# Batched matrix product on one core: output stores gathered into groups of up to four

## The chip, the cores and the metric

The kernel runs on one core of one Trainium2 chip. The metric is the device time of one launch in microseconds (us), given as the median of several runs. Before the change it is 511.59 us (three runs, 511.37 to 511.65).

The core has five instruction streams: PE (TensorE, matrix products and transposes), DVE (VectorE), ACT (ScalarE), POOL (GpSimd) and SP (SyncE). Transfers between the main memory and the on-chip memory run on 16 DMA engines; POOL and SP put them into queues, and the transfers of one queue are worked through in the order of issue.

## The reference

```python
def setup_inputs():
    batch, m, k, n = 32, 512, 1024, 768
    return {
        "x": np.random.randn(batch, m, k).astype(np.float32),
        "weight": np.random.randn(batch, k, n).astype(np.float32),
    }

def reference(x: np.ndarray, weight: np.ndarray) -> np.ndarray:
    return np.matmul(x, weight).astype(np.float32)
```

There are 32 independent products of 512x1024 by 1024x768. In float32, x is 67.1 MB, weight 100.7 MB and the output 50.3 MB; each byte crosses the memory interface once.

## The kernel before

**Pairs.** The 32 batches are worked in 16 pairs; pair k holds batches 2k and 2k+1. The x of a pair is one transfer of 4.19 MB read (`load_x`, line 111), which POOL issues and which turns float32 into bfloat16 on its way. The weights of a pair are 6.29 MB read, also turned into bfloat16: where `together(b)` holds, one transfer brings both batches (line 98), otherwise there is one transfer for each batch (line 102). The output of a pair is one store of 3.15 MB (`store`, line 119). Store a is the output of pair a.

**Buffers.** There are four slots for weights (two pairs), two for x and four for outputs (`W_SLOTS, X_SLOTS, OUT_SLOTS = 4, 2, 4`). Output slot a % 4 is filled by pair a and is free for pair a + 4 when store a has landed. ACT asks for that (`slot_free`) before the first copy of a pair.

**PE.** For each pair PE transposes the x (`transposes`, line 173, with copies by DVE on lines 219 and 227), then multiplies batch 2k and batch 2k+1 (`multiply`, lines 138 and 165), each in four blocks of 128 rows. A block can only begin when ACT and DVE have emptied the accumulators that it writes (lines 261, 265, 270 and 272). DVE makes its last copy of a pair only behind the transposes of the next pair.

**POOL's order.** POOL's program, `on_pool`, is a plain list. Each step may wait, and everything behind it waits too:

```python
for k in range(PAIRS - 2):
    load_x(k + 2)
    if k % 2 == 0:
        stores(k - 3, k - 1)
    load_w(2 * k + 4)
    load_w(2 * k + 5)
stores(PAIRS - 3 - HELD, PAIRS - 2)
```

`load_x(k + 2)` waits until the first block of pair k is multiplied, since it reuses that pair's x buffer. `stores(first, last)` issues stores first to last-1; each waits for the last copies of its pair. A weight transfer of two batches waits until both batches of pair k are multiplied; one for a single batch waits for one batch. Stores 11, 12 and 13 come at the end of the list. The outputs of the last two pairs are stored by SP: pair 14 in one transfer, batches 30 and 31 in one of half the size each (line 123).

Of the kernel before, what the change touches and what calls it, by code (L numbers as in the profile page):

```python
# [12 lines left out]
def kernel(  # L13
# [7 lines left out]
    B, M, K = x.shape  # L21
# [6 lines left out]
    N2 = 2 * N  # L28
    ROW = MT * N
    PAIRS = B // 2  # L30
    HELD = 2
    GROUPS = 2 * MT
    W_SLOTS, X_SLOTS, OUT_SLOTS = 4, 2, 4

# [53 lines left out]


    def together(b):  # L90
        return W_SLOTS <= b < B - 2

    def load_w(b):
        if together(b):
            if b % 2 == 0:
                pool.wait_ge(s_mm, mm_done(b + 1 - W_SLOTS))
                slots = all_ws[:, b // 2 % 2].rearrange("p r ko n -> p r (ko n)")
                pool.dma_start(out=slots, in_=w_two_view[b // 2]).then_inc(s_w[b % W_SLOTS], 16)  # L98
            return
        if b >= W_SLOTS:  # L100
            pool.wait_ge(s_mm, mm_done(b - W_SLOTS))
        pool.dma_start(out=ws[b % W_SLOTS], in_=w_view[b]).then_inc(s_w[b % W_SLOTS], 16)  # L102

    def loads_of_w(b):

        return sum(not (together(i) and i % 2) for i in range(b % W_SLOTS, b + 1, W_SLOTS))

    def load_x(k):
        if k >= X_SLOTS:
            pool.wait_ge(s_mm, mm_begun(k - X_SLOTS))  # L110
        pool.dma_start(out=xs[k % X_SLOTS], in_=x_view[k]).then_inc(s_x[k % X_SLOTS], 16)  # L111
# [5 lines left out]
    def store(eng, a, sem):  # L117
        copied(eng, 4 * a + 3)
        eng.dma_start(out=two_view[a], in_=outs[a % OUT_SLOTS]).then_inc(sem, 16)  # L119
# [219 lines left out]
    def on_pool():  # L339
        pool.dma_start(out=xs[0][:, MT:], in_=x_view[0, :, MT:]).then_inc(s_rest, 16)  # L340
        load_w(0)
        pool.memset(ident, 0.0).then_inc(s_zero, 1)  # L342
        pool.wait_ge(s_zero, 1)
        pool.affine_select(  # L344
            out=ident,
            in_=ident,
            compare_op=mybir.AluOpType.not_equal,
            fill=1.0,
            base=0,
            pattern=[[-1, P]],  # L350
            channel_multiplier=1,
        ).then_inc(s_ident, 1)
        load_w(1)
        load_x(1)
        load_w(2)
        load_w(3)
        def stores(first, last):
            for a in range(max(first, 0), last):
                store(pool, a, s_st[a % OUT_SLOTS])


        for k in range(PAIRS - 2):
            load_x(k + 2)
            if k % 2 == 0:
                stores(k - 3, k - 1)
            load_w(2 * k + 4)
            load_w(2 * k + 5)
        stores(PAIRS - 3 - HELD, PAIRS - 2)

    def on_sp():  # L370
        for b in range(B):
            if b == 0:
                sp.wait_ge(s_cast, 2).then_inc(s_xr, 1)
            elif b % 2 == 0:
                k = b // 2
                landed(sp, s_x[k % X_SLOTS], (k + 1) // X_SLOTS, s_xr)
            if not (together(b) and b % 2):
                landed(sp, s_w[b % W_SLOTS], loads_of_w(b), s_wr, 1 + together(b))
        store(sp, PAIRS - 2, s_fin)
        store_one(B - 2)  # L380
        store_one(B - 1)
        sp.sem_inc(s_zero, 1)
# [12 lines left out]
    with tc.tile_critical(sync_engine=mybir.EngineType.Activation, no_gpsimd_drain=True):  # L395
        on_pool()
        tc.wait_critical_data_deps()
        on_pe()
        on_dve()
        on_act()  # L400
        on_sp()
        clear_on_pool()
# [30 lines left out]
```

## Time and profile before

| what | value |
|---|---|
| median of the runs | 511.59 us (511.37 to 511.65) |
| span of the profiled execution | 509.6 us, first to last instruction |
| median less that span | 2.0 us, which lie outside the recorded instructions |
| PE, DVE, ACT, POOL busy | 84%, 42%, 22%, 6% of the span |
| transfers issued by POOL | 16 of x, 19 of weights, 14 stores |
| transfers issued by SP | half of the first x, 3 stores |

The profiled execution is given by its span. The profile's busy share of PE is modelled and is not the share of its peak. DMA share is the mean busy share of the 16 DMA engines; since packets overlap a little on an engine, it can read slightly above 1. The view of issues gives, for each transfer, the time from its issue to its landing: a transfer that stands behind others in the queue has their time in it. The moment of landing is the start of the issue in the timeline plus that time.

### The profile page before, as it was taken

To read this page: it belongs to the slowest core of one execution; us is meant where nothing else is said; L and a number is where in the kernel's file an instruction comes from. 1 tells how busy PE (TensorE), PEld (TensorE's weight loads), DVE (VectorE), ACT (ScalarE), POOL (GpSimd) and SP (SyncE) were. 2 spreads that over 40 slices of the span, in tenths; PEclk is the share of its full clock that TensorE was granted. 3 is DMA by queue.
4 is the path that set the end of the run, shared out by engine and by line. 5 is a ranking of instruction groups with operands and counts; after the bars stand their busy time and mean duration, and the time that the engine had idled before them with its cause. 6 is when DMAs were issued, how large, how long until landed. Compare 5 with 4: busy or idle time off the path is not lost. (4 is left out here: it accounts for less than half of the span.)

```text
span 509.6 us, 5832 instructions
## 1 busy us (share of the span) xinstructions
PE 429.4 (84%) x2560; PEld 172.8 (34%) x1536; DVE 211.7 (42%) x330; ACT 114.1 (22%) x195; POOL 29.6 (6%) x55
## 2 busy tenths in 40 slices
PE   0899989999899399993999949999399994999990
PEld 0525342443325034250343513434034341433420
DVE  1436362454635136351373514635146351454631
ACT  1131312223130231302313023230231302223230
POOL 3000000000101001010010100100001000100000
PEclk9999998999999799996999979999699997999996
DMA  8999999999999999999999999999999999999998
GB/s 262 216 211 216 225 207 221 215 305 247 221 212 230 432 234 214 217 237 432 226 215 217 247 433 216 218 217 259 420 217 217 219 267 408 218 215 229 432 430 347
DMA packets 9299, 135.29 MB, mean 266 GB/s; under 512 B 848, under 2 KB 848, under 8 KB 848
## 3 DMA queue, kind: packets, MB, share of 16 engines
q0 software_dynamic: 8720, 126.88, 96.8%
q1 hardware_dynamic: 576, 8.39, 4.0%
q14 instruction: 3, 0.02, 0.0%
HBM read 167.77 MB, written 50.33 MB: 428 GB/s over the span
## 5 line engine op out<-in xcount | busy, mean ns | idle before, releaser
L165 PE MATMUL pm<-w,xT 128*128 x1024 | 346.2, 389 | 42.0 <-DVE outs L270 38.7
L138 PE MATMUL pm<-w,xT 128*128 x1024 | 284.7, 278 | 0.0
L165 PEld LDWEIGHTS pm<-w,xT 128*128 128x128 bf16 x1024 | 102.3, 100 | 282.8 <-issue 241.0
L270 DVE COPY outs<-pm 64x512 f32<-64x512 f32 x128 | 88.2, 689 | 207.7 <-DVEq L268 206.3
L261 ACT COPY outs<-pm 64x512 f32<-64x512 f32 x128 | 74.2, 580 | 272.6 <-PE pm L138 168.4
L173 PE MATMUL pt<-ident,x 128*128 128x128 f32 x512 | 84.5, 307 | 24.8 <-PEq L177 14.5
L219 DVE COPY xT<-pt 128x1024 bf16<-128x1024 bf16 x120 | 77.7, 687 | 63.9 <-PE pt L173 63.6
L173 PEld LDWEIGHTS pt<-ident,x 128*128 128x128 f32 x512 | 71.2, 210 | 40.0 <-DVE xT L219 18.8
L265 ACT COPY outs<-pm 64x512 f32<-64x512 f32 x64 | 37.0, 579 | 99.5 <-PE pm L138 99.3
L272 DVE COPY outs<-pm 64x512 f32<-64x512 f32 x64 | 43.9, 686 | 0.0
L98 POOL DMA_DIRECT2D w<-in_weight_dram x13 | 9.2, 708 | 264.6 <-PE pm L138 264.6
L111 POOL DMA_DIRECT2D x<-in_x_dram x15 | 8.4, 557 | 123.2 <-PE pm L138 92.4
L119 POOL DMA_DIRECT2D out_dram<-outs x14 | 7.5, 539 | 7.1 <-DVE outs L272 7.1
L227 DVE COPY xT<-pt 128x512 bf16<-128x512 bf16 x16 | 5.7, 418 | 4.1 <-PE pt L173 4.1
L280 DVE CAST x<-outs 128x1024 bf16<-128x1024 f32 x2 | 1.3, 692 | 11.0 <-DMA outs<-in_x_dram 11.0
L102 POOL DMA_DIRECT2D w<-in_weight_dram x6 | 3.2, 544 | 26.5 <-PE pm L138 26.3
L280 ACT ACT_TABLE_LOAD x1 | 1.3, 1283 | 10.7 <-DMA outs<-in_x_dram 10.7
L280 ACT CAST x<-outs 128x1024 bf16<-128x1024 f32 x2 | 2.0, 1042 | 0.0
L340 POOL DMA_DIRECT2D x<-in_x_dram x1 | 0.7, 670 | 0.8 <-POOLq L417 0.8
L344 POOL TENSOR_SCALAR_AFFINE_SELECT ident<-ident 128x128 f32<-128x128 f32 x1 | 0.3, 284 | 0.2 <-POOL ident L342 0.2
L342 POOL MEMSET ident<- 128x128 f32 x1 | 0.2, 232 | 0.0
L417 POOL MEMSET const-float32-0.0<- 128x1 f32 x1 | 0.1, 99 | 0.2 <-issue 0.2
(3 smaller groups left out, 0.3 us busy)
## 6 DMA issues: line engine op xcount, KB each, us to landing
out_dram<-outs POOLq DMA_DIRECT2D x14, 3072.0 KB, 40.1
w<-in_weight_dram POOLq DMA_DIRECT2D x13, 3072.0 KB, 32.9
x<-in_x_dram POOLq DMA_DIRECT2D x15, 2048.0 KB, 34.3
w<-in_weight_dram POOLq DMA_DIRECT2D x6, 1536.0 KB, 30.5
out_dram<-outs SPq DMA_DIRECT2D x1, 3072.0 KB, 18.7
out_dram<-outs SPq DMA_DIRECT2D x2, 1536.0 KB, 13.6
outs<-in_x_dram SPq DMA_DIRECT2D x1, 2048.0 KB, 9.7
x<-in_x_dram POOLq DMA_DIRECT2D x1, 1024.0 KB, 11.6
```

Of the source, the lines that this page charges most:

```text
L98: pool.dma_start(out=slots, in_=w_two_view[b // 2]).then_inc(s_w[b % W_SLOTS], 16)
L111: pool.dma_start(out=xs[k % X_SLOTS], in_=x_view[k]).then_inc(s_x[k % X_SLOTS], 16)
L119: eng.dma_start(out=two_view[a], in_=outs[a % OUT_SLOTS]).then_inc(sem, 16)
L138: return pe.add_instruction(mybir.InstMatmult(name=nc.get_next_instruction_name(), engine=mybir.EngineType.PE, ins=[pe.lower_ap(moving), p ...
L165: last = pe.matmul(*args, start=(ko == 0), stop=(ko == KT - 1))
L173: last = pe.transpose(pts[g % 2][:, j, :], words[:, mo, j::JT], ident)
L219: return dve.tensor_copy(both[g // 2][:, :, :, g % 2].rearrange("p b j i r -> p j b i r"), pt)
L227: last = dve.tensor_copy(rows, pt[:, :, b])
L261: last = act.copy(*piece)
L265: act.copy(*pieces(b, p, 2)[0]).then_inc(s_ap, 1)
L270: last = dve.tensor_copy(*piece)
L272: dve.tensor_copy(*pieces(b, p, 2)[1]).then_inc(s_dp, 1)
```

## The change

The groups of stores behind the x loads are no longer one or two stores in every second step but three or four in steps 2, 6 and 10 (behind the x of pairs 4, 8 and 12). In these steps the weights are loaded batch by batch. Slots, waits, sizes, the computation and all engines but POOL are as they were; SP's waits for weights count the added transfers.

```diff
-    HELD = 2
+    STORED_AT = (2, 6, 10)
@@
     def together(b):
-        return W_SLOTS <= b < B - 2
+        return W_SLOTS <= b < B - 2 and b // 2 - 2 not in STORED_AT
@@
         for k in range(PAIRS - 2):
             load_x(k + 2)
-            if k % 2 == 0:
-                stores(k - 3, k - 1)
+            if k in STORED_AT:
+                stores(k - 3, k + 1)
             load_w(2 * k + 4)
             load_w(2 * k + 5)
-        stores(PAIRS - 3 - HELD, PAIRS - 2)
+        stores(STORED_AT[-1] + 1, PAIRS - 2)
```

The end of the list issues stores 11, 12 and 13 in both versions.

On POOL, in the middle of the program, the transfers before stand as follows. The first line is the x of pair 8 and the last the x of pair 10; x0 and x1 are the two x buffers, `out_0_dram` is the output in main memory, and a weight transfer of 128x2x6144 is one of two batches.

```order
L111 DMA x0<-in_x_dram 128x8192
L119 DMA out_0_dram<-outs 128x6144 x2
L98 DMA w<-in_weight_dram 128x2x6144
L111 DMA x1<-in_x_dram 128x8192
L98 DMA w<-in_weight_dram 128x2x6144
L111 DMA x0<-in_x_dram 128x8192
```

In the changed program the same place, from the x of pair 8 to the x of pair 10, reads:

```order
L111 DMA x0<-in_x_dram 128x8192
L119 DMA out_0_dram<-outs 128x6144 x4
L102 DMA w<-in_weight_dram 128x6144 x2
L111 DMA x1<-in_x_dram 128x8192
L98 DMA w<-in_weight_dram 128x2x6144
L111 DMA x0<-in_x_dram 128x8192
```

Stores 5 and 6 have joined stores 3 and 4, and the weights of pair 8 behind them are two transfers of one batch in place of one of two. In the next place, from the x of pair 10 to the x of pair 12, the program before has two stores:

```order
L111 DMA x0<-in_x_dram 128x8192
L119 DMA out_0_dram<-outs 128x6144 x2
L98 DMA w<-in_weight_dram 128x2x6144
L111 DMA x1<-in_x_dram 128x8192
L98 DMA w<-in_weight_dram 128x2x6144
L111 DMA x0<-in_x_dram 128x8192
```

The changed program has none there:

```order
L111 DMA x0<-in_x_dram 128x8192
L98 DMA w<-in_weight_dram 128x2x6144
L111 DMA x1<-in_x_dram 128x8192
L98 DMA w<-in_weight_dram 128x2x6144
L111 DMA x0<-in_x_dram 128x8192
```

So the groups of stores in POOL's list are 0 | 1, 2 | 3, 4 | 5, 6 | 7, 8 | 9, 10 | 11 to 13 before, and 0 to 2 | 3 to 6 | 7 to 10 | 11 to 13 now. The other engines' programs stand in the same order as before.

## Prediction

> **What bounds the kernel now.** I read the page's top first, then the stretches of time, then POOL's timeline with the times to landing.
>
> ```profile
> span 509.6 us, 5832 instructions
> DMA  8999999999999999999999999999999999999998
> q0 software_dynamic: 8720, 126.88, 96.8%
> HBM read 167.77 MB, written 50.33 MB: 428 GB/s over the span
> ```
>
> The row of DMA digits is 9 in all but the first and last slice: the 16 DMA engines are never idle for long. They carry 167.77 + 50.33 = 218.10 MB. The stretches show it more sharply (the last two columns are the DMA share and the bytes written per time; loads count half there, since they turn float32 into bfloat16; the column ahead of them is PE's granted clock).
>
> ```profile
> 2.00:100.00 98.00, 82.20 (x488) 34.13 (x296) 39.49 (x60) 24.14 (x39) 7.42 (x14) 0.98 1.02 226
> 100.00:200.00 100.00, 87.68 (x529) 36.73 (x325) 45.90 (x71) 21.92 (x38) 5.92 (x10) 0.97 1.01 262
> 200.00:300.00 100.00, 84.25 (x504) 33.32 (x299) 39.29 (x60) 19.78 (x35) 5.45 (x10) 0.94 1.02 267
> 300.00:400.00 100.00, 88.42 (x517) 34.44 (x307) 43.27 (x66) 24.62 (x44) 5.93 (x10) 0.92 1.02 260
> 400.00:500.00 100.00, 86.86 (x524) 34.18 (x309) 43.78 (x74) 23.59 (x41) 3.94 (x7) 0.96 1.01 310
> 500.00:507.00 7.00, 0.00 (x0) 0.00 (x0) 0.00 (x0) 0.00 (x0) 0.00 (x0) 0.50 1.01 432
> 507.00:510.00 3.00, 0.00 (x0) 0.00 (x0) 0.00 (x0) 0.00 (x0) 0.00 (x0) 0.50 0.09 37
> ```
>
> The share is 1.01 or 1.02 from 2 us to 507 us, through store groups and load stretches alike, and 0.09 of the last 3 us (0.3 us): the engines work from about 2 us to 507.3 us without a hole. PE, DVE and ACT all wait in between and lie beside that. So the time is bytes by rate, plus 2 us ahead and 2 us behind. A new order of the same bytes can change it in three ways only: the switch from loads to stores and back may cost something, a transfer may cost something of its own, or the queue may run dry.
>
> **The switch from loads to stores.** The change takes three of the seven groups of POOL's stores away (seven become four). What a group costs is read from landings. POOL's issues (start, length, what):
>
> ```profile
> 69.19 0.71 POOL L98 DMA_DIRECT2D w<-in_weight_dram  x1 [17.65 <-PE pm L138]
> 99.25 0.71 POOL L98 DMA_DIRECT2D w<-in_weight_dram  x1 [17.09 <-PE pm L138]
> 107.53 0.56 POOL L111 DMA_DIRECT2D x<-in_x_dram  x1 [7.57 <-PE pm L138]
> 125.74 0.71 POOL L98 DMA_DIRECT2D w<-in_weight_dram  x1 [17.65 <-PE pm L138]
> 153.88 0.71 POOL L98 DMA_DIRECT2D w<-in_weight_dram  x1 [16.58 <-PE pm L138]
> 162.16 0.56 POOL L111 DMA_DIRECT2D x<-in_x_dram  x1 [7.56 <-PE pm L138]
> 190.53 0.71 POOL L98 DMA_DIRECT2D w<-in_weight_dram  x1 [27.81 <-PE pm L138]
> 198.95 0.56 POOL L111 DMA_DIRECT2D x<-in_x_dram  x1 [7.71 <-DVE outs L272]
> 199.50 1.07 POOL L119 DMA_DIRECT2D out_dram<-outs  x2
> 254.49 0.71 POOL L98 DMA_DIRECT2D w<-in_weight_dram  x1 [28.51 <-PE pm L138]
> ```
>
> The times to landing of the first seven of these, in the same order (last column, us):
>
> ```profile
> w<-in_weight_dram POOLq DMA_DIRECT2D x1, 3072.0 KB, 30.9
> w<-in_weight_dram POOLq DMA_DIRECT2D x1, 3072.0 KB, 32.9
> x<-in_x_dram POOLq DMA_DIRECT2D x1, 2048.0 KB, 34.3
> w<-in_weight_dram POOLq DMA_DIRECT2D x1, 3072.0 KB, 30.7
> w<-in_weight_dram POOLq DMA_DIRECT2D x1, 3072.0 KB, 41.3
> x<-in_x_dram POOLq DMA_DIRECT2D x1, 2048.0 KB, 42.7
> w<-in_weight_dram POOLq DMA_DIRECT2D x1, 3072.0 KB, 28.9
> ```
>
> The weights of pairs 3, 4, 5, 6 and 7 land at 100.1, 132.2, 156.4, 195.2 and 219.4 us, the x of pairs 5 and 7 at 141.8 and 204.9. With nothing but loads ahead of it, x takes 204.9 - 195.2 = 9.7 us and a pair's weights 156.4 - 141.8 = 14.6, together 24.3. From 156.4 to 219.4 are 63.0 us; two pairs' loads take 48.6 of them, and stores 1 and 2 the other 14.4, which is 7.2 each. A long run of stores without loads stands at the end:
>
> ```profile
> 488.04 10.72 SPq L123 DMA_DIRECT2D out_dram<-outs  x2
> out_dram<-outs SPq DMA_DIRECT2D x1, 1536.0 KB, 10.2
> ```
>
> The second of these issues starts at 488.04 + 10.72 - 0.34 = 498.4 (0.34 being the length of SP's one other store issue, so an estimate) and lands at 508.6. Batch 31's weights land at 472.2 (row below). In the 36.4 us between lie stores 11 to 14 and two halves, five stores' worth: 7.28 each. So a group of two with both its switches costs 14.4 - 2 x 7.28 = -0.2 us: nothing. The dearest group is the first: 132.2 - 100.1 - 24.3 = 7.8 us for store 0 alone, 0.5 more than 7.28. Three groups fewer is thus worth between +0.5 us (3 x 0.16 lost) and -1.5 us (3 x 0.5 gained). I take 0, since all the groups taken away are ones of two, like the first row. The third and fourth store of a row cost what the others do, by the run of five.
>
> **A transfer's own cost.** Three transfers of two batches become six of one, so 22 weight transfers in place of 19. At the end of the program before, two single ones stand next to each other:
>
> ```profile
> 415.68 0.56 POOL L111 DMA_DIRECT2D x<-in_x_dram  x1 [7.57 <-PE pm L138]
> 432.70 0.53 POOL L102 DMA_DIRECT2D w<-in_weight_dram  x1 [16.46 <-PE pm L138]
> 443.10 0.53 POOL L102 DMA_DIRECT2D w<-in_weight_dram  x1 [9.86 <-PE pm L138]
> x<-in_x_dram POOLq DMA_DIRECT2D x1, 2048.0 KB, 41.7
> w<-in_weight_dram POOLq DMA_DIRECT2D x1, 1536.0 KB, 32.0
> w<-in_weight_dram POOLq DMA_DIRECT2D x1, 1536.0 KB, 29.1
> ```
>
> They land at 464.7 and 472.2, behind the x at 457.4: 14.8 us for both against 14.6 for a pair. The bounds are 0 and 3 x 0.2 = +0.6 us; I take 0, because the landings are rounded to 0.1 and the difference is of that size. POOL itself issues for 6 x 0.53 - 3 x 0.71 = 1.1 us more, beside a full queue. The Trainium skill, "DMA: Bandwidth & Descriptors", section "Anatomy of one DMA — SWDGE (gpsimd) path", gives each transfer from this queue about 2.0 us of fixed cost on top of its bytes and says that most of it is the wait until the last byte is confirmed. Were that paid in the queue, three more transfers would make the time 6 us longer, an estimate of 517.6; the landings here, 14.8 against 14.6 us, say that it is hidden behind the transfers that follow.
>
> **Can the queue run dry?** POOL's list is in order, so the last store of a group, whose pair has just been multiplied, now holds back both weight transfers and the next x. Take the second group. The rows are these (DVE's last copy of pair 6; ACT's waits for store slots; PE's clock while it waits):
>
> ```profile
> 224.60 0.69 DVE L272 COPY outs<-pm 64x512 f32<-64x512 f32 x1
> ACT outs L261 <- DMA out_dram<-outs: 103.4, 6, 19.2
> 234.00:238.00 4.00, 0.00 (x0) 0.00 (x0) 1.18 (x2) 1.36 (x3) 0.00 (x0) 0.50 1.03 442
> ```
>
> Up to the x of pair 8 the same bytes stand in the queue in both kernels, so pair 7's weights still land at 219.4 and the x of pair 8 at 229.1. Stores 3 to 5 are issued behind it at about 200 us, and store 6 at 225.3, when DVE's copy ends. By 7.28 us each, stores 3 to 6 land at 236.4, 243.7, 250.9 and 258.2; batches 16 and 17 (7.3 each) at 265.5 and 272.8; the x of pair 9 at 282.5. When store 6 is issued the queue still has work up to store 5's landing, 250.9 - 225.3 = 25.6 us. Pair 7 waits for store 3 as it did, so pair 9's weights are issued at 254.5 as in the row above, 28 us ahead of the queue's end. A pair's multiplying is read from POOL's rows: the x issue at 107.53 waits for the first block of pair 3, the weight issue at 125.74 for its eighth, so seven blocks take 18.2 us, one 2.6 and a pair 20.8. Pair 8 starts at 265.5 with the weights of batch 16 (those of batch 17 are there before it gets to them) and ends at 286.3, or 289 with a cold clock. The weights of pair 10 then find the x of pair 10 ahead of them, up to 306.8: 18 to 20 us left. Pair 9 starts with its weights at 297.1 and ends by about 318 to 321, the x of pair 11 ending at 331: 10 to 13 us left, the least of the cycle. Before, the least is 28.9 - 14.6 = 14.3 us. So the queue never empties; cost 0. The clock falls to 0.50 while PE waits, as it already does; a cold start costs some 3 us of PE (an estimate: about 6 us at half speed), which these margins hold.
>
> Where does PE's stall go? Pairs 5, 9 and 13 no longer wait for a store to free their slot, pairs 7, 11 and 15 still do; pairs 8 and 12 wait longer for weights instead. PE still has to wait for the same bytes.
>
> **The tail.** Stores 11 to 15 and the last loads keep their order. SP's last issue at 498.4 finds 10.2 - 3.64 (its own half) - 1.3 (508.6 less 507.3, the landing's delay) = 5.3 us of work ahead of it. Now pair 13 waits for weights, two stores later than before: an estimated 423.4 us, and 20.8 us of multiplying bring it to 444.2, against 443.1 in the row of the last weight issue. That is 1.1 us of the 5.3; cost 0.
>
> **Sum.** 509.6 + 0 (switches) + 0 (transfers) + 0 (queue) + 0 (tail) = 509.6 us of span. The median of the runs stands 2.0 above the span, so 511.6 us; no change.
>
> **The rivals.**
>
> *Switches do cost.* If each group taken away had cost what the first one did, 3 x 0.5 = 1.5 us go: 510.1 us. For it speaks only that first group; against it the group of stores 1 and 2, which costs nothing measurable.
>
> *PE is late at the end (slower).* Place: pairs 12 and 13, which now wait for weights with the clock down. It decides from 5.3 us of delay on; each further us is one of time. With two cold starts of 3 us more than I counted, 1.1 + 6 = 7.1, so 1.8 us too late: 513.4 us. For it speaks the clock of 0.50 in the row above; against it that pair 13's transposes should end before its weights come.
>
> *Each transfer costs on its own.* Three times 0.2 us: 512.2 us, which is under what counts as a difference.
>
> *Long runs of stores are slower.* If the third and fourth store of a row (2, 5, 6, 9 and 10) each cost 0.5 us more, as store 0 did: 514.1 us. Against it stand five in a row at 7.28.
>
> *The change does not do what it says:* excluded, since POOL's list shows the groups.
>
> **How the numbers follow.** Forecast 0.80, switches cost 0.08, PE late 0.06, transfers cost 0.03, long runs 0.03. A difference of 0.2% (1.0 us) is what a measurement of this kernel can tell from none. Faster: 0.08. Slower: 0.06 + 0.03 = 0.09. Same: 0.80 + 0.03 = 0.83. The terms of the forecast reach from 511.6 - 1.5 to 511.6 + 0.5 + 0.6 at their bounds; I give 510.6 to 512.4, which leaves out the far end of the switches, the late PE and the long runs.
>
> **What would show it.** The DMA share stays at 1.01 or so in each stretch to 507 us, and the time from pair 7's weights to pair 9's is their loads and four stores of 7.28. ACT's waits for stores fall from six to three, about 46 us (two of 19 and a short one), with no gain in the span. Wrong would be: a share under 0.98 in any stretch of 100 us (the queue ran dry), a weight landing behind a group earlier than the bytes say by 0.5 us or more (switches cost), or a last issue on SP after 503 us (the tail is PE's).

## The result and the profile after

| | before | changed |
|---|---|---|
| median | 511.88 us (11 runs, 511.37 to 512.44) | 513.21 us (11 runs, 512.81 to 513.28) |
| ratio to before | | 1.0023 (95% interval 1.0015 to 1.0031) |
| span of the profiled execution | 509.6 us | 511.1 us |

The change makes the kernel slower by 1.3 us. The forecast was 511.6 us, no change, range 510.6 to 512.4: wrong, the time is 1.6 us above it and outside the range.

The page of the changed kernel, the lines that answer to those shown of before:

```profile
span 511.1 us, 5790 instructions
DMA  9999999999999999999999999999999999999996
q0 software_dynamic: 8768, 126.88, 96.5%
HBM read 167.77 MB, written 50.33 MB: 427 GB/s over the span
```

The same bytes, and DMA engines busy nearly throughout. The stretches of the changed kernel (DMA share in the last column but one):

```profile
2.00:100.00 98.00, 81.42 (x479) 34.26 (x296) 39.45 (x60) 24.15 (x39) 7.25 (x14) 0.98 1.02 226
100.00:200.00 100.00, 85.11 (x496) 36.09 (x314) 43.49 (x68) 20.86 (x36) 5.37 (x9) 0.93 1.01 262
200.00:300.00 100.00, 83.52 (x478) 33.14 (x292) 41.70 (x64) 20.77 (x36) 6.25 (x11) 0.93 1.01 279
300.00:400.00 100.00, 85.96 (x494) 33.81 (x298) 39.28 (x60) 21.92 (x38) 6.81 (x12) 0.92 1.02 279
400.00:500.00 100.00, 94.38 (x568) 36.86 (x336) 45.74 (x77) 26.09 (x45) 3.92 (x7) 0.98 1.01 279
500.00:507.00 7.00, 0.68 (x5) 0.10 (x1) 1.99 (x3) 0.58 (x1) 0.00 (x0) 0.75 0.96 406
```

Up to 500 us nothing is lost: 1.01 or 1.02, as before. The difference is in the last microseconds. The last stretches of the kernel before, then of the changed one:

```profile
505.00:507.00 2.00, 0.00 (x0) 0.00 (x0) 0.00 (x0) 0.00 (x0) 0.00 (x0) 0.50 1.01 430
507.00:508.00 1.00, 0.00 (x0) 0.00 (x0) 0.00 (x0) 0.00 (x0) 0.00 (x0) 0.50 0.26 111
508.00:509.00 1.00, 0.00 (x0) 0.00 (x0) 0.00 (x0) 0.00 (x0) 0.00 (x0) 0.50 0.00 0
```

```profile
503.00:505.00 2.00, 0.00 (x0) 0.00 (x0) 0.00 (x0) 0.00 (x0) 0.00 (x0) 0.63 0.92 387
505.00:507.00 2.00, 0.00 (x0) 0.00 (x0) 0.00 (x0) 0.00 (x0) 0.00 (x0) 0.50 0.97 406
507.00:508.00 1.00, 0.00 (x0) 0.00 (x0) 0.00 (x0) 0.00 (x0) 0.00 (x0) 0.50 0.53 221
508.00:509.00 1.00, 0.00 (x0) 0.00 (x0) 0.00 (x0) 0.00 (x0) 0.00 (x0) 0.50 0.06 25
509.00:510.00 1.00, 0.00 (x0) 0.00 (x0) 0.00 (x0) 0.00 (x0) 0.00 (x0) 0.50 0.03 12
```

A share of 0.06 is 1/16: from 508 to 509.5 us a single one of the 16 DMA engines is at work, and everything waits for it. A transfer is split over 16 engines, each of which reports its own end; the trace keeps all 16 ends. The landing that the view of issues gives, and for which the program waits, is the last of them. Let the *lag* be that last end less the median of the 16. For the last transfer of all, batch 31's store:

```
kernel     median of the 16 ends    last of the 16 ends    lag
before     507.75 us                508.65 us              0.89 us
changed    507.94 us                510.16 us              2.22 us
```

The median moved by 0.19 us, the lag by 1.33: together 1.52, the difference of the spans (511.08 - 509.56). In the changed kernel 14 engines end within 0.1 us of the median, one 0.7 us behind it and one 2.2: that one makes the loss.

How does it get late? The trace has each packet's duration. A store packet of 24576 bytes takes 912 ns. In the second group of stores some take 926 to 973, and they follow each other at the step of one engine's packets:

```
store packets of 919 ns or more (start in us: ns), 229.2 us to the end of the group
before   240.2:931
changed  236.1:932 237.0:926 237.9:935 238.8:935 239.8:940 241.6:926 242.5:926
         243.5:953 244.4:935 245.3:945 246.3:931 247.2:935 248.1:926 249.1:954
         250.0:973 251.0:953 251.9:926 252.8:931 253.8:954 254.7:945 255.7:935
         and five of 966 to 1107 ns from 256.6 on
```

The 21 are 0.56 us over 912 in all, and the lag grows in this group from 0.23 to 0.92 us. It is not made good afterwards: the lag reads 0.92 us at 273 us and still at 356 us. The lag was 0.17 us at 100 us, and 1.51 after the third group (before: 0.19 and 0.56 at the same times). In the last run of stores it grows once more, from 1.52 to 2.22; before, it is 0.88 at the start of that run and 0.89 at its end.

What PE does while stores pass is the other difference. The windows of the second group, before (two stores, columns as in the prediction) and then changed (four stores):

```profile
229.00:236.00 7.00, 1.32 (x9) 0.29 (x3) 0.00 (x0) 0.00 (x0) 0.00 (x0) 0.83 0.99 428
236.00:244.00 8.00, 5.65 (x19) 1.41 (x10) 2.16 (x4) 3.06 (x6) 0.00 (x0) 0.51 1.02 399
```

```profile
229.00:236.00 7.00, 5.14 (x32) 1.47 (x15) 0.11 (x1) 0.00 (x0) 2.13 (x4) 1.00 1.03 442
236.00:244.00 8.00, 5.38 (x17) 1.38 (x10) 2.12 (x4) 3.01 (x6) 0.00 (x0) 0.58 0.99 424
244.00:251.00 7.00, 6.95 (x44) 2.10 (x22) 3.49 (x6) 2.11 (x4) 0.00 (x0) 0.99 0.98 421
251.00:258.00 7.00, 6.51 (x43) 3.85 (x32) 2.98 (x6) 1.74 (x3) 0.71 (x1) 1.00 1.04 420
```

Before, PE stands still for most of the group, since pair 7 waits for store 3 to free its slot. In the changed kernel it stands only until store 3 has landed and multiplies while stores 4, 5 and 6 pass. ACT's waits for stores (total, times, longest) say the same for the whole run, 103.4 us in six waits before:

```profile
ACT outs L261 <- DMA out_dram<-outs: 30.5, 2, 15.3
```

### The profile page after: what moved, and what is told of

It is laid out like the page before. It is cut to its first block, busy times and chain, and to the rows that moved or that the text cites. A ratio compares the mean times of both kernels' runs of the same rounds, so it can differ in the third digit from the quotient of the medians.

```text
span 511.1 us, 5790 instructions
## 1 busy us (share of the span) xinstructions
PE 431.1 (84%) x2512; PEld 174.3 (34%) x1536; DVE 211.7 (41%) x330; ACT 114.4 (22%) x195; POOL 30.6 (6%) x58
## 5 line engine op out<-in xcount | busy, mean ns | idle before, releaser
L165 PEld LDWEIGHTS pm<-w,xT 128*128 128x128 bf16 x1024 | 103.4, 101 | 286.0 <-issue 275.8
L98 POOL DMA_DIRECT2D w<-in_weight_dram x10 | 7.0, 705 | 184.8 <-PE pm L138 184.8
L102 POOL DMA_DIRECT2D w<-in_weight_dram x12 | 6.5, 552 | 17.2 <-PE pm L138 17.1
```

Of the source, the lines that this page charges most:

```text
L165: last = pe.matmul(*args, start=(ko == 0), stop=(ko == KT - 1))
```

## The experiments

Three theories were on trial. **A**: one engine is slower in long runs of stores. **B**: the added transfers cost. **C** or **P**: POOL is held, or PE is late at the end. Theory **M** came from the first eight runs: one engine's stores are slower whenever PE multiplies. (In the counts below, PE's work means its matrix instructions, products and transposes alike.) All are compared with the kernel before on the same chip.

**Only the split weights.**

```diff
+    SPLIT_AT = (2, 6, 10)
-        return W_SLOTS <= b < B - 2
+        return W_SLOTS <= b < B - 2 and b // 2 - 2 not in SPLIT_AT
```

> The kernel before with the weights of pairs 4, 8 and 12 loaded batch by batch; the stores stay in groups of one and two. Theory A (one of the 16 DMA engines works through stores a few per cent slower once stores have followed stores for some 7 us, and its lag is never made good, so the last landing moves while the mean of the 16 does not): no change, ratio 0.9990 to 1.0007, and few slow store packets in the middle of the run. Theory B (three more weight transfers cost): about as slow as the change, ratio 1.0015 to 1.0030.

511.92 us, ratio 0.9998 (0.9989 to 1.0007). The added transfers cost nothing: B falls.

**Only the groups.**

```diff
-        return W_SLOTS <= b < B - 2 and b // 2 - 2 not in STORED_AT
+        return W_SLOTS <= b < B - 2
```

> The change with all weights in transfers of two batches, as before; the stores in groups of three and four. Theory A: as slow as the change, ratio 1.0015 to 1.0031, with one engine's store packets at 926 to 954 ns instead of 912 from the second store of each group on. Theory B: no change, 0.999 to 1.0007. Theory C (POOL held at the group's last store makes PE late at the end): slower than the change, since the weights of pairs 8 and 12 come still later.

513.76 us, ratio 1.0037 (1.0023 to 1.0051). The groups alone make the lag: 1.04 us at 290 us and 1.82 at 416. The time of this kernel, though, is not the lag's. It is slower than the change, as C said, and for C's reason: the last copy of DVE ends at 505.6 us, the engines run dry ahead of the last store, and its 16 ends lie close together (the last 0.08 us behind their median).

```profile
503.00:505.00 2.00, 0.37 (x3) 0.00 (x0) 1.42 (x3) 0.58 (x1) 0.00 (x0) 1.00 0.34 141
505.00:507.00 2.00, 0.00 (x0) 0.00 (x0) 0.56 (x1) 0.00 (x0) 0.00 (x0) 0.94 0.42 178
```

**The stores of a group in two runs of two.**

```diff
             if k in STORED_AT:
-                stores(k - 3, k + 1)
+                stores(k - 3, k - 1)
             load_w(2 * k + 4)
+            if k in STORED_AT:
+                stores(k - 1, k + 1)
             load_w(2 * k + 5)
```

> The change with the same stores in the same three steps, but the weights of the first batch put between the second and the third store, so that no more than two stores follow each other ahead of the end. Theory A: about as before, ratio 0.9990 to 1.0008, the lag of the slowest engine at the last weight landing back to under 1 us. Theories B and C (three more transfers; POOL held at the group's last store): still slow, 1.0015 to 1.003.

513.36 us, ratio 1.0028 (1.0018 to 1.0038), where A said no change. The lag is 1.23 us at 290 us and 2.74 at 473; 0.9 us of the latter came with one weight packet of 1836 ns instead of 926 at 375.5 us. So A as first put falls: a run need not be long for the loss.

**One store in each step.**

```diff
-            if k % 2 == 0:
-                stores(k - 3, k - 1)
+            stores(k - 1, k)
...
-        stores(PAIRS - 3 - HELD, PAIRS - 2)
+        stores(PAIRS - 3, PAIRS - 2)
```

> The kernel before with one store in each step, that of the pair before (store k-1 in step k), and only store 13 at the end of POOL's list: no store follows another until the last weights are in, and the run of stores at the end is three stores' worth long instead of five. Theory A: a little faster than before, by 0.4 to 0.8 us, ratio 0.9984 to 0.9994. If switches between loads and stores cost (as few tenths of a us each), it is slower than before: 8 groups more at up to 0.5 us, ratio up to 1.008.

516.72 us, ratio 1.0098 (1.0079 to 1.0116), where A said faster. Two things show. No pair waits for a store any more, so PE multiplies in all of the stores' time; there are 13 switches from loads to stores ahead of the last loads, and the lag is 3.68 us at 475 us. And stores 11 and 12 now stand ahead of the last weights, so PE ends later: the share falls to 0.03 ahead of the last store. That lateness sets the time of this kernel, since the last store's 16 ends lie together (the last 0.08 us behind their median).

```profile
505.00:507.00 2.00, 1.29 (x8) 0.29 (x3) 0.52 (x1) 0.58 (x1) 0.00 (x0) 1.00 0.17 74
507.00:508.00 1.00, 0.00 (x0) 0.00 (x0) 0.99 (x3) 0.00 (x0) 0.00 (x0) 1.00 0.03 12
```

**Half of the products left out**, in the kernel before, in the change, and in the kernel with one store in each step:

```diff
-        for ko in range(KT):
+        for ko in range(0, KT, 2):
...
-                    last = other(*args, ko == 0, ko == KT - 1)
+                    last = other(*args, ko == 0, ko == KT - 2)
...
-                    last = pe.matmul(*args, start=(ko == 0), stop=(ko == KT - 1))
+                    last = pe.matmul(*args, start=(ko == 0), stop=(ko == KT - 2))
```

> The kernel before with every second slice of the inner dimension left out of the products (half of the matrix multiplications; all transfers as they were), so that PE cannot be late anywhere. A base for the next two. If the time is bytes by rate, it stays within 0.3% of the kernel before: 511 to 512 us.

> The change with the same half of the products left out. Theory A (one or two DMA engines fall behind through long runs of stores and end last, whatever PE does): 1.0 to 1.5 us above the light kernel before. Theory P (PE is late at the end, so the last store is issued too late): as the light kernel before, within 0.3 us.

> The kernel with one store in each step, with the same half of the products left out. Theory P: as the light kernel before, within 0.5 us, since its 4.9 us were PE's lateness. Theory A with a loss on single engines at each switch from loads to stores (the slowest engine was 3.7 us behind the median at the last weights): still 2 to 3 us above the light kernel before.

Measured: 512.51 (510.97 to 513.49), 512.11 and 513.86 us. With a light PE the change costs nothing against its own base. That is what P expected and A did not; but leaving products out also takes away PE's work beside the stores, so these runs don't part P from M. The packets do, within one group of the light change (0 to 2). PE multiplies until 121 us and then stands:

```profile
110.00:121.00 11.00, 9.18 (x55) 5.55 (x44) 7.55 (x12) 3.10 (x6) 0.71 (x1) 1.00 1.00 431
121.00:130.00 9.00, 0.00 (x0) 0.00 (x0) 2.07 (x4) 0.00 (x0) 0.00 (x0) 0.71 1.01 434
```

Its store packets of 919 ns or more (start in us: ns) end with PE's work at 120.4 us; in the second window there is none, and one more comes at 130.8 us, while PE still stands:

```
113.3:942 114.2:940 115.2:945 116.1:935 117.0:952 118.0:954 118.9:935 119.9:954 130.8:936
```

The third kernel keeps 1.35 us over the first, with a lag of 3.16 us at the end: PE's lateness was the larger part of its loss, but not all.

**The first two groups of the change, then twos as before.**

```diff
-    STORED_AT = (2, 6, 10)
+    STORED_AT = {2: (0, 3), 6: (3, 7), 10: (7, 9), 12: (9, 11)}
+    SPLIT_AT = (2, 6)
...
-        return W_SLOTS <= b < B - 2 and b // 2 - 2 not in STORED_AT
+        return W_SLOTS <= b < B - 2 and b // 2 - 2 not in SPLIT_AT
...
-                stores(k - 3, k + 1)
+                stores(*STORED_AT[k])
...
-        stores(STORED_AT[-1] + 1, PAIRS - 2)
+        stores(11, PAIRS - 2)
```

> The change with only its first two groups (stores 0 to 2 and 3 to 6); from store 7 on grouped in twos as before, so that pair 13 waits for a store again and not for weights. Full products. Theory P: no change against before, 0.9990 to 1.0007, the last copy by DVE back at about 498 us. Theory A: about half of the change's loss, ratio 1.0008 to 1.0018, with a slowest engine some 1 us behind at the last weights.

513.17 us, ratio 1.0024 (1.0015 to 1.0033), with PE nearly as early as before (last copy of DVE at 500.2 us against 498.4). So P falls as the cause of the change's loss. But the loss is the whole one, not half: the lag is 1.40 us at 457 us and jumps to 2.43 by 473, with one weight packet of 2004 ns instead of 926 just ahead of the stores (470.5 us). Why all ten runs lose the whole (512.87 to 513.49 us), and not the one profiled alone, stays open.

**Groups of two, none of which a pair waits for.** The decisive run: lengths, switches and the end are those of before.

```diff
-                stores(k - 3, k - 1)
+                stores(k - 2, min(k, 11))
```

> The kernel before with the same steps for its stores, but each group one store further on (0 and 1 in step 2, 2 and 3 in step 4, up to 8 and 9 in step 10, 10 alone in step 12, 11 to 13 at the end). No pair has to wait for a store to free its slot, so PE multiplies while most stores pass; runs of stores are no longer than before and the end is the same. Theory A as first put (the slow engine comes from long runs of stores): no change, 0.9990 to 1.0007. Theory M (one engine's store packets take 926 to 954 ns instead of 912 whenever PE multiplies, and the kernel before hides this since PE stands still, waiting for a slot, while its stores pass): slower than before by 0.6 to 1.5 us, ratio 1.0012 to 1.0030, with ACT's waits for stores near zero and more slow packets in the groups of two.

513.43 us, ratio 1.0036 (1.0023 to 1.0048): M's sign, and a little over its range. ACT waits once; PE multiplies all through the third group; the lag at the end is 3.08 us (0.4 of it came with one x packet of 1640 ns instead of 1227 at 298.1 us), its median end at 507.39. The wait, and two windows:

```profile
ACT outs L261 <- DMA out_dram<-outs: 9.9, 1, 9.9
```

```profile
236.00:244.00 8.00, 7.95 (x50) 2.45 (x25) 3.87 (x6) 2.32 (x4) 0.00 (x0) 1.00 1.02 439
244.00:251.00 7.00, 6.95 (x44) 2.05 (x22) 2.08 (x4) 2.90 (x5) 0.00 (x0) 1.00 0.97 381
```

From 239.8 to 250.1 us this kernel has 12 slow store packets, where the kernel before has one in a group of the same length. The group starts at 235.4 us: its first four microseconds have none, though PE is at work.

**The needed store last.**

```diff
-                stores(k - 3, k + 1)
+                first = k - 2 if k == 6 else k - 3
+                stores(first, k + 1)
+                stores(k - 3, first)
```

> The change with the second group's stores issued in the order 4, 5, 6, 3, so that pair 7 waits for the last of the four instead of the first and PE stands still through nearly all of that group. Theory A as first put: as the change, slowest engine some 0.9 us behind the median after that group. Theory M: few slow packets from 229 to 258 us, the slowest engine under 0.5 us behind at 265 us, and 0.3 to 0.6 us less than the change in all, unless PE is then late at the end (last copy by DVE later than about 503 us).

PE stands through the second group but for its first 7 us:

```profile
236.00:244.00 8.00, 0.00 (x0) 0.00 (x0) 0.00 (x0) 0.00 (x0) 0.00 (x0) 0.68 0.97 418
244.00:251.00 7.00, 0.00 (x0) 0.00 (x0) 0.00 (x0) 0.00 (x0) 0.00 (x0) 0.50 1.02 439
251.00:258.00 7.00, 0.00 (x0) 0.00 (x0) 0.00 (x0) 0.00 (x0) 0.00 (x0) 0.50 1.03 418
```

Four stores in a row, and the lag behind them is 0.39 us, as it was ahead of them (0.38), against 0.92 and 1.05 in the two profiles of the change. That is M's figure and not A's. In all it is slower, 515.14 us, ratio 1.0055 (1.0041 to 1.0069). DVE's last copy ends at 505.0 us, as in the exception that the expectation named, but this is not where the time went. The median of the 16 ends is 3.2 us later than in the change already at the last weights (474.37 us against 471.19), and 2.9 us later at the end. It was lost in the middle: pair 7's wait held back POOL's next weight issue from 254.65 to 276.82 us, and later the queue ran empty (share 0.57).

```profile
328.00:331.00 3.00, 2.70 (x20) 1.48 (x13) 0.79 (x2) 0.88 (x2) 0.71 (x1) 1.00 0.57 120
```

So of this run only the lag tests M; the time does not.

**Repeats.** The change and the kernel before, unchanged.

> The change once more, to see how far the lag of the slowest engine repeats from one profiled execution to the next. Theories A and M: slow store packets in the second and third group again, the slowest engine 1.0 to 2.0 us behind the median at 447 us, span 510.8 to 511.5 us. If the lag were chance, it would differ as much as between kernels.

> The kernel before once more, for the same reason: few slow packets between 165 and 435 us, the slowest engine 0.5 to 1.0 us behind at 447 us, span 509.4 to 510.0 us.

The change: 513.04 us, ratio 1.0026 (1.0016 to 1.0035); the kernel before: 511.87 us in its one run. The lag is no chance of one execution, as these counts from the packets show. (Slow: store packets of 919 to 990 ns between 100 and 465 us, without those of 925, which all engines have on the first store packet behind a load. Time: microseconds in which at least 12 store packets start, by whether a matrix instruction of PE starts in them too. Lags: at the last load that had landed by 290.5, 416 and 458.6 us, and at the end.)

```
kernel                  span   slow  PE at work/standing  lag 290  416   458   end
before                  509.6   20        44 / 34          0.26   0.54  0.69  0.89
before, again           509.8   22        50 / 32          0.61   1.00  1.15  1.29
split weights only      509.7   18        37 / 40          0.46   0.63  1.02  1.32
change                  511.1   85        72 /  8          0.92   1.51  1.51  2.22
change, again           511.0   68        71 /  9          1.05   1.65  1.65  2.23
twos without a wait     511.4   64        82 /  0          0.90   2.13  2.17  3.08
change, light           509.9   37        44 / 35          0.28   0.68  0.68  1.08
before, light           510.6    5        27 / 52          0.74   1.98  1.97  2.00
```

Over all 14 profiles, to the end of each, a slow packet starts in 785 of 1213 such microseconds with PE at work and in 33 of 294 without. The packets don't follow PE to the microsecond: in the second group of the change PE stands from 234.1 to 238.4 us, and the slow ones start at 236.1. And M leaves out one condition. With PE at work throughout, slow packets start in 1 of the 24 microseconds that are the first four of a group in the kernel of twos without a wait, and in 12 of 52 with one store in each step; from the sixth microsecond on in 50 of 52 and 23 of 24. A run of stores must have lasted some four microseconds.

The last row shows what M doesn't cover: there the lag rose from 0.94 to 2.02 us in two steps without slow store packets, the larger (0.8 us) with an x packet of 1908 ns instead of 1227 at 353.3 us, just ahead of a group. By slow packets alone the light change should have been the slower of the two; it measured 0.4 us less.

## Why the prediction was wrong, point by point

**The failed step** is "The third and fourth store of a row cost what the others do, by the run of five", and behind it the sentence that a new order can change the time "in three ways only". The term was taken as 0 and measured 1.3 us. It is not the third or fourth place as such that costs: in a run of stores that has lasted some four microseconds, one of the 16 engines takes some 3% longer for store packets while PE works, about 0.2 us in a store (eight packets of 912 ns and 25 to 30 ns more on each). The kernel before had a cover against this: its groups are short, and PE stood, waiting for a slot, in 34 of the 78 microseconds of stores counted above. The change took away "PE's stall", which the prediction set down as of no account ("PE still has to wait for the same bytes"), and with it the cover.

The run of five that was to prove the price has the slow packets too, 27 of them in the kernel before and 26 in the changed one (0.8 us over 912 in each); measured from a last end to a last end, it did not show them. The trace says why: followed back packet by packet, the engine that has them starts this run at 470.77 us in the kernel before, ahead of the median of the 16 starts (470.99), and the lag of 0.88 us at its start is another engine's. In the changed kernel it starts last of all, at 472.37 us against a median of 470.87, and its slow packets come on top of that. So about half of the 1.33 us was picked up in the middle, and the other half is a price that the kernel before paid on an engine that had it to spare.

**The rival that came nearest** is "Long runs of stores are slower", 514.1 us at a chance of 0.03. Its sign and size were about right, and its mechanism was not: four stores in a row with PE standing cost no lag, two in a row with PE at work do. What is right in it is that the first store of a row, with PE at work, is the cheaper one.

**Switches, added transfers.** Both terms of 0 stand for the rate of the engines together: the split weights alone measure 0.9998, and the median end of the last store moved by 0.19 us with three groups fewer. But single engines lose up to a microsecond in load packets ahead of stores (2004 ns instead of 926 in the run with the tail as before), which the prediction's last-landing arithmetic could not see; that the switch causes it is not shown.

**The queue** never ran dry up to 500 us, as worked out. Store 6 was issued at 229.67 us instead of 225.3, which did no harm: store 5, ahead of it in the queue, landed only at 251.5.

**The tail** was mis-sized. Forecast: 1.1 us of PE's lateness out of a margin of 5.3. The last copies of DVE, before and changed:

```profile
497.67 0.69 DVE L272 COPY outs<-pm 64x512 f32<-64x512 f32 x1
```

```profile
502.18 0.69 DVE L272 COPY outs<-pm 64x512 f32<-64x512 f32 x1
```

It is 4.5 us: pair 13's weights land on the slowest engine at 424.2, and the first block is done only at about 429, at the reduced clock (0.66 from 424 to 429 us). The margin all but held: the share of 0.92 between 503 and 505 us is what is seen of it, and the median end gives it at most 0.19 us.

**Waits for stores** fell further than the three and 46 us forecast, to two and 30.5, since pair 15 came too late to wait.

## What to carry to other kernels

Here, where the DMA engines were full from end to end, the time was that of the slowest of the 16, and a lag that this one had picked up was still there at the end. So compare the share of the last microseconds (0.06 is one engine of 16) ahead of any cost per transfer. Ask also whose lag it is: one price hurt on the engine that was last and cost nothing on one that was ahead. A stall of an engine that is not the bound may be doing something useful: here it kept PE's work away from the stores. And stores held back to the end were worth something: with one store in each step, which puts two more of them ahead of the last loads, DVE's last copy ended at 508.5 us instead of 498.4.

## What was not expected of the hardware

One engine takes 926 to 973 ns for store packets of 24576 bytes, where the others take 912, mostly while PE works and seldom while it stands (785 of 1213 microseconds against 33 of 294), and hardly in the first four microseconds of a run of stores. In the last store run of the change it is so for packets of POOL's queue (9 from 484 to 500 us) and of SP's (8). The Trainium skill, "DMA: Bandwidth & Descriptors", section "Latency and other measured facts", says that two certain engines are usually slower than the rest and gives as its best guess a crowded port, through which all engines fetch the descriptors that POOL's transfers keep in on-chip memory. That one engine is slower agrees; that SP's packets on it are slow too doesn't decide on the guess, since all of them run beside POOL's. The trace names no engine, so whether it is one of those two stays open.

Single load packets just ahead of a store group took up to 2202 ns (x, in the light kernel with one store in each step, at 210.9 us) instead of 1227; such jumps differ from run to run and are not explained. Also open is why PE's work slows a store, and whether the profiler's own records take part in it. The copies that go with the products were not tested apart. By the busy shares of the 14 profiles a slow packet starts in 107 of 225 microseconds with PE busy more than half and no copy by DVE or ACT, in 21 of 61 with copies (over 0.3) and no PE, and in 8 of 208 with neither; so PE's work without copies is enough, but copies may do it too.
